# One order function for two phase changes of a hybrid encoder block on one Trainium2 core

## The chip, the cores and the metric

The kernel runs on one core of a Trainium2 chip. A core has five engines that run side by side, each with a queue of its own that it works off in order: TensorE (PE, the matrix unit; its weight loads are shown apart as PEld), VectorE (DVE), ScalarE (ACT), GpSimd (POOL) and SyncE (SP, which here issues the transfers). The metric is device time of one execution in microseconds (us). The kernel before took 1838.58 us, the median of three runs (1838.55 to 1839.45).

## The reference

One layer on 256 rows of width 2048: a half-weighted SwiGLU feed-forward part (FFN), a token mixer, and a second FFN, each with a modulated norm in front and a gated norm behind.

```python
h = modulate(rms_norm(x, ffn1_pre_g), sh1, sc1)
y = swiglu(h, ffn1_w_gu, ffn1_w_down)               # 2048 -> 2*5504 -> 2048
x = x + 0.5 * gt1 * rms_norm(y, ffn1_post_g)

h = modulate(rms_norm(x, mix_pre_g), sh2, sc2)
proj = h @ w_in                                     # q, k, v, u_b, v_b
out_a, out_b = band_attention(q, k, v), spatial_gating(u_b, v_b)
merged = concat(rms_norm(out_a, g_out_a), rms_norm(out_b, g_out_b))
y = merged @ w_out
x = x + gt2 * rms_norm(y, mix_post_g)

h = modulate(rms_norm(x, ffn2_pre_g), sh3, sc3)
x = x + 0.5 * gt3 * rms_norm(swiglu(h, ffn2_w_gu, ffn2_w_down), ffn2_post_g)
```

The modulation vectors (shift, scale and gate for each of the three parts) come from a product of a conditioning vector with `w_ada`.

## The kernel before

All products are made in split precision: an fp32 operand is split into a high part (`hi`, a cast on ScalarE) and the rest (`lo`, a subtraction on VectorE), and `mm3` (L111) issues three matmuls, high by high (L113), high by low (L114), low by high (L115). Weights stream in through `load` (L117, 1 MB each, three raw buffers) and `split` (L152), which puts each half of a load, a k-tile, into the next of a cyclic list of slots (`use_slots`, L138). A slot is free again when TensorE has used its k-tile for both tiles of rows. The 256 rows are two tiles, t = 0 and 1, of 128 rows. `h`, the normed and modulated input of a part, is split in the same way into hhi and hlo.

A phase change lies at the end of FFN 1 (`down_last`, L455, with `finish1`, L723) and at the end of the mixer's out-projection (L1007 to L1030). There the following has to happen for each tile of rows, in this order:

- TensorE ends the tile's last banks of `dn` (FFN 1) or `wo` (mixer). There are four banks of 512 columns per tile in FFN 1, of which each takes nine matmuls, and in the mixer two banks at the end, after two that were evacuated earlier.
- `evac` or `evac_b` adds a bank to `y` on VectorE (L479, L983). `y_done` (L296) squares it on ScalarE with its sum (L171) and multiplies it, in place, by the gate vector on VectorE (L303). In place, the product waits until the square has read `y`.
- `rstd` (L173) adds the sums on VectorE (ms) and takes the power on GpSimd (r).
- `post` (L309): four updates `x += y * r` on VectorE (L314) and four squares of x on ScalarE.
- `pre` (L271): again ms and r, then `dg`, a diagonal matrix of r (L277). TensorE transposes and scales x in four groups (`xtp`, L281). For each group VectorE makes the first quarter of h (L290) and ScalarE the other three (L288); then ScalarE makes hhi and VectorE hlo (L268, L269). Two PSUM banks hold the groups, so the third group waits until the first has been read.

Only then can TensorE begin the next product for that tile: `pj` (in-projection, `in_pair`, L736) or `gu` (FFN 2, `lead_chunk`, L356). For these, tile 0 leads: it takes eight k-tiles before tile 1 starts with the first (`LEAD`, L322). Some k-tiles of the next weight are split ahead, during the last matmuls of the phase before: six of `w_in` (`ahead1`, L708), five of `w_gu2` (L1017).

The order of the instructions on each engine is set by a scheduler at compile time: of the instructions that it believes ready, it takes the one of highest priority. `tc.high_priority()` raises that of the phase change. `after` (L125) adds an order between two instructions of one engine, and `order["split"]` holds pairs of instructions behind which the next splits have to stand (L160, L161):

```python
if t == 0:
    order["split"] += [(i_sq, i_x)] * 2        # post
...
if t == 0:
    order["split"] += [inst] * 2               # pre, for each group
```

Of the kernel before, what the change touches and what calls it, by code (L numbers as in the profile page):

```python
# [12 lines left out]
F32 = mybir.dt.float32  # L13
# [5 lines left out]
P = 128  # L19
# [43 lines left out]
def block_kernel(ctx: ExitStack, tc: tile.TileContext, a: dict, out: bass.AP):  # L63
# [46 lines left out]

    def mm3(ps, st, mv, start, stop):  # L111
        (ah, al), (wh, wl) = st, mv
        nc.tensor.matmul(ps, ah, wh, start=start, stop=False)  # L113
        nc.tensor.matmul(ps, ah, wl, start=False, stop=False)  # L114
        nc.tensor.matmul(ps, al, wh, start=False, stop=stop)  # L115

    def load(src, off, n):  # L117
        raw = wraw.tile([P, 2048], F32, tag="raw", name=nm("raw"))
# [1 line left out]
        return raw  # L120


    order = {"ada": (None, 0), "split": []}

    def after(inst, first):  # L125

# [25 lines left out]
    def split(raw):  # L152
        n = raw.shape[1]
        hi, lo = slot()
        i_hi = nc.scalar.copy(hi[:, :n], raw)  # L155
        i_lo = nc.vector.tensor_tensor(lo[:, :n], raw, hi[:, :n].bitcast(F32), op=ALU.subtract)  # L156
        order["last"] = (i_hi, i_lo)
        if order["split"]:
# [109 lines left out]
        i_hi = nc.scalar.copy(hi, h32)  # L268
        return i_hi, nc.vector.tensor_tensor(lo, h32, hi.bitcast(F32), op=ALU.subtract)  # L269

    def pre(i, x, t, ssq, h):  # L271

        hi, lo = h
        r = rstd(ssq)
        ts = slice(t * P, (t + 1) * P)
        dg = sm.tile([P, P], F32, tag="xn", name=nm("dg"), bufs=2)
        nc.vector.tensor_scalar(dg, ident, r, None, op0=ALU.mult)  # L277
        for j in range(4):
            ps = ptr.tile([P, 4, P], F32, tag="tr", name=nm("xtp"))
            for q in range(4):  # L280
                nc.tensor.matmul(ps[:, q, :], x[t][:, (4 * j + q) * P:(4 * j + q + 1) * P], dg, start=True, stop=True)  # L281
            h32 = sm.tile([P, 4, P], F32, tag="h32", name=nm("h32"), bufs=2)
            for q in range(4):
                kt = 4 * j + q
                g1 = gmul[:, i * KT + kt:i * KT + kt + 1]
                s1 = mod[:, SH[i] * KT + kt:SH[i] * KT + kt + 1]
                if q:
                    nc.scalar.activation(h32[:, q, :], ps[:, q, :], AF.Identity, bias=s1, scale=g1)  # L288
                else:
                    nc.vector.tensor_scalar(h32[:, q, :], ps[:, q, :], g1, s1, op0=ALU.mult, op1=ALU.add)  # L290
            inst = split_act(h32, hi[:, 4 * j:4 * j + 4, ts], lo[:, 4 * j:4 * j + 4, ts])
            if t == 0:
                order["split"] += [inst] * 2
        order["ada"] = (inst[1], 2)

    def y_done(t, n, y, ysq, g, junk, behind=None):  # L296

        ns = slice(n * CH, (n + 1) * CH)
        inst = square(junk, y[t][:, ns], ysq[t], n, D)
        if behind:  # L300
            after(inst, behind[0])
        r = rstd(ysq[t]) if n == 3 else None
        nc.vector.tensor_tensor(y[t][:, ns], y[t][:, ns], g[0][:, ns], op=ALU.mult)  # L303
        return r

    def new_ysq():
        return [new_sums("ysq", 4) for _ in range(NT)]

    def post(x, t, y, r):  # L309

        xsq = new_sums("xsq", 4)
        for j in range(4):
            js = slice(j * CH, (j + 1) * CH)
            i_x = nc.vector.scalar_tensor_tensor(out=x[t][:, js], in0=y[t][:, js], scalar=r, in1=x[t][:, js], op0=ALU.mult, op1=ALU.add)  # L314
            junk = sm.tile([P, CH], F32, tag="xn", name=nm("junk"), bufs=2)
            i_sq = square(junk, x[t][:, js], xsq, j, D)
        if t == 0:
            order["split"] += [(i_sq, i_x)] * 2
        return xsq


    LEAD = 8  # L322
# [1 line left out]
    def ffn(wgu, wdn, h, avp, ahp, plan, rate, gate_of, finish, lead=(), after_lead=(), ahead=None):  # L324
# [130 lines left out]
        def down_last(c, g):  # L455

            off, w = CHUNKS[c]
            nk = w // P
            ysq = new_ysq()
            blocks = []  # L460
            tail = ahead is None
            for i in range(nk):
                raw = load(wdn, D * off + i * P * 2048, 2048)
                tick()
                for q in range(2):
                    wh, wl = split(raw[:, q * 1024:(q + 1) * 1024])
                    blocks += [(wh[:, :CH], wl[:, :CH]), (wh[:, CH:], wl[:, CH:])]
            if not tail:
                ahead()

            def mm(t, n):
                ps = pmm.tile([P, CH], F32, tag="mm", name=nm("dn"))
                for k in range(nk):
                    mm3(ps, (stat[c][t][0][:, k, :], stat[c][t][1][:, k, :]), blocks[n * nk + k], k == 0, k == nk - 1)
                return ps

            def evac(t, n, ps):
                ns = slice(n * CH, (n + 1) * CH)
                nc.vector.tensor_tensor(y[t][:, ns], y[t][:, ns], ps, op=ALU.add)  # L479
                return y_done(t, n, y, ysq, g, avp.tile([P, CH], F32, tag="av", name=nm("junk"), bufs=2))  # L480

            with tc.high_priority():
                for n in range(4):
                    r = evac(0, n, mm(0, n))
                late = [mm(1, n) for n in range(4)]
                if not tail:
                    finish(0, y, r)
                for n in range(4):
                    r1 = evac(1, n, late[n])
                if tail:  # L490
                    finish(0, y, r)
                finish(1, y, r1)

        todo, ready = [], []
        if plan:
# [206 lines left out]
    h2, x1, sp1 = [], [], []  # L702
    if True:
        avp, gp = Lazy(tc, wx, "av1", 2), Lazy(tc, wx, "gp1", 1)
        ahs = ExitStack()
        ahp = Lazy(tc, ahs, "ah1", 2, lambda: (avp.open(), gp.open()))

        def ahead1():  # L708

            ahs.close()  # L710
            pre = wx.enter_context(tc.tile_pool(name="pre1", bufs=2))
            rest = ((adap, 2), (pre, 2), (wsp, 4), (wx1, 3))
            use_slots(*rest, once=((wx1, 1),) + rest)
            for _ in range(3):
                sp1.extend(in_visit())

        def gate1():
            flush_ada(SH[1])
            gain(1, 0, KT)
            x1.extend(load_x(a["x"]))  # L720
            return gate(0, 0.5, gp)

        def finish1(t, y, r):  # L723
            if not h2:
                h2.extend(new_h())
# [144 lines left out]
    with tc.tile_pool(name="bp", bufs=1) as bp:  # L870
# [74 lines left out]
        def wo_mm(ps, m, sp, kt, t, bs=(0, 1)):  # L945
            for b in bs:
                mv = (sp[0][:, b * CH:(b + 1) * CH], sp[1][:, b * CH:(b + 1) * CH])
                ts = slice(t * P, (t + 1) * P)
                mm3(ps[b][t], (m[0][:, kt, ts], m[1][:, kt, ts]), mv, kt == 0, kt == 7)
# [28 lines left out]
    with tc.tile_pool(name="gp2", bufs=1) as gp:  # L978
        ysq = new_ysq()

        def evac_b(t, n, ps, behind=None):
            ns = slice(n * CH, (n + 1) * CH)
            inst = nc.vector.scalar_tensor_tensor(out=y[t][:, ns], in0=ps, scalar=rb[t], in1=y[t][:, ns], op0=ALU.mult, op1=ALU.add)  # L983
            if behind:
                after(inst, behind[1])
            return y_done(t, n, y, ysq, g, sm.tile([P, CH], F32, tag="xn", name=nm("junk"), bufs=2), behind)

        use_slots((wsp, 4), (wx2, 3))
        g = []
# [17 lines left out]
        ps = wo_banks()  # L1007
        for kt in range(4):
            wo_mm(ps, m_b, sp[kt], kt, 0)
        sp += wo_visit() + wo_visit()  # L1010
        for b in range(2):
            for kt in range(4, 8):
                wo_mm(ps, m_b, sp[kt], kt, 0, (b,))

        use_slots((wsp, 1), once=((adap, 1), (wsp, 4)))
        sp3 = []
# [3 lines left out]
        for kt in range(4):  # L1020
            wo_mm(ps, m_b, sp[kt], kt, 1)
        for b in range(2):
            for kt in range(4, 8):
                wo_mm(ps, m_b, sp[kt], kt, 1, (b,))
        h3.extend(new_h())
        with tc.high_priority():
            for t in range(NT):
                for b in range(2):
                    r = evac_b(t, 2 + b, ps[b][t])
                pre(2, x2, t, post(x2, t, y, r), h3)  # L1030
    mxs.close()
    wx3 = ctx.enter_context(tc.tile_pool(name="wx3", bufs=3))

# [1 line left out]
    with ExitStack() as ahs:  # L1035
# [13 lines left out]
        def finish3(t, y, r):  # L1049
            for j in range(4):  # L1050
                js = slice(j * CH, (j + 1) * CH)
                nc.vector.scalar_tensor_tensor(out=x2[t][:, js], in0=y[t][:, js], scalar=r, in1=x2[t][:, js], op0=ALU.mult, op1=ALU.add)
# [79 lines left out]
```

## Time and profile before

| | |
|---|---|
| median of three runs | 1838.58 us |
| the profiled execution's own time | 1839.32 us |
| its span, first to last instruction | 1837.2 us |
| busy: PE, DVE, ACT, POOL | 1803.2, 1328.4, 854.5, 31.3 us |
| first phase change: last `dn` matmul, first `pj` matmul | 745.62, 752.78 us |
| second phase change: last `wo` matmul, first `gu` matmul | 1102.16, 1108.48 us |
| last `dn` matmul of FFN 2 | 1826.49 us |

The profile is of one execution, and its times count from the first instruction. Busy time of TensorE counts a matmul from its issue to its modelled end, and successive matmuls overlap. A row of the order of time gives start, duration, engine, line, operation, output and inputs with shapes, and how many instructions of the kind were merged; in square brackets stands for how long the engine was idle before, and what ended that.

### The profile page before, as it was taken

How to read it: one execution, taken by the hardware profiler on the slowest of the kernel's cores; microseconds unless marked ns; L12 is line 12 of the kernel's file. 1: busy time of each engine (PE TensorE's matmuls, PEld its weight loads, DVE VectorE, ACT ScalarE, POOL GpSimd, SP SyncE). 2: the span in 40 equal slices, each digit the busy share in tenths (PEclk: the TensorE clock that was granted, in tenths of full speed). 3: DMA queues.
4: the chain of work that ended last, by engine and by line, in shares of the span. 5: the costliest groups of instructions: out<-in, count | busy, mean ns of one | idle time of the engine just before them, and what ended most of it. 6: DMA issues, size and time to landing. Idle time of an engine off the chain costs nothing.

```text
span 1837.2 us, 21286 instructions
## 1 busy us (share of the span) xinstructions
PE 1803.2 (98%) x8271; PEld 1501.1 (82%) x8271; DVE 1328.4 (72%) x1481; ACT 854.5 (47%) x1105; POOL 31.3 (2%) x59
## 2 busy tenths in 40 slices
PE   7999999999999999999999999999999999999997
PEld 6777788888888898788888887888888888888896
DVE  7989998988877876768789986774445445445456
ACT  6544354444443344645555557444443443443342
POOL 0000000000000000000001000000000000000000
PEclk9999999999999999999999999999999999999999
DMA  9988788898888876479788974875555555555461
GB/s 395 385 335 318 286 320 342 326 367 332 336 335 321 329 289 261 172 276 358 292 307 326 382 291 165 332 305 187 195 191 187 196 191 187 196 190 186 160 250 70
DMA packets 71477, 499.11 MB, mean 272 GB/s; under 512 B 7968, under 2 KB 8144, under 8 KB 13136
## 3 DMA queue, kind: packets, MB, share of 16 engines
q1 hardware_dynamic: 70560, 492.48, 70.2%
q0 software_dynamic: 720, 5.24, 0.7%
q8 instruction: 65, 1.06, 0.2%
q14 instruction: 36, 0.29, 0.0%
q10 hardware_dynamic: 96, 0.02, 0.0%
HBM read 493.50 MB, written 4.22 MB: 271 GB/s over the span
## 4 chain that ended last, share of the span: by engine, by line
PE 93%; DVE 4%; ACT 1%; issue 1%; DMA 0%; POOL 0%; POOLq 0%; DVEq 0%; SPq 0%; ACTq 0%
PE gu L114 16%; PE gu L115 16%; PE gu L113 16%; PE dn L113 8%; PE dn L114 8%; PE dn L115 8%; PE pj L113 4%; PE pj L115 4%; PE pj L114 4%; PE wo L113 1%; PE wo L115 1%; PE wo L114 1%; DVE lo L156 1%; PE atp L418 1%; PE xtp L281 1%
## 5 line engine op out<-in xcount | busy, mean ns | idle before, releaser
L155 ACT CAST hi<-raw 128x1024 fp32r<-128x1024 f32 (+1 forms) x628 | 645.9, 1042 | 811.5 <-PE gu L115 422.6
L156 DVE TENSOR_TENSOR lo<-raw,hi 128x1024 fp32r<-128x1024 f32 (+1 forms) x628 | 747.8, 1208 | 380.9 <-ACT hi L155 379.5
L113 PE MATMUL gu<-hi,hhi 128*128 128x512 f32 (+1 forms) x1396 | 536.8, 387 | 8.9 <-DVE acc L392 4.2
L114 PE MATMUL gu<-lo,hhi 128*128 128x512 f32 (+1 forms) x1396 | 537.9, 385 | 0.4 <-DVE lo L156 0.3
L115 PE MATMUL gu<-hi,hlo 128*128 128x512 f32 (+1 forms) x1396 | 537.7, 385 | 0.0
L202 DVE CUSTOM_DVE_ANT_0 ada<-ada,c_bc,small 128x2048 f32<-128x2048 f32 x144 | 337.4, 2344 | 9.6 <-PE qkt L797 9.0
L113 PEld LDWEIGHTS gu<-hi,hhi 128*128 128x128 f32 x1396 | 262.4, 188 | 62.4 <-ACT hi L155 5.2
L114 PEld LDWEIGHTS gu<-lo,hhi 128*128 128x128 f32 x1396 | 263.0, 188 | 50.3 <-DVE lo L156 1.2
L115 PEld LDWEIGHTS gu<-hi,hlo 128*128 128x128 f32 x1396 | 262.9, 188 | 50.0
L113 PE MATMUL dn<-hi,ah 128*128 128x512 f32 x640 | 249.2, 389 | 0.0
L114 PE MATMUL dn<-lo,ah 128*128 128x512 f32 x640 | 249.0, 389 | 0.0
L115 PE MATMUL dn<-hi,al 128*128 128x512 f32 x640 | 249.0, 389 | 0.0
L113 PEld LDWEIGHTS dn<-hi,ah 128*128 128x128 f32 x640 | 120.1, 188 | 25.1
L115 PEld LDWEIGHTS dn<-hi,al 128*128 128x128 f32 x640 | 120.1, 188 | 25.0
L114 PEld LDWEIGHTS dn<-lo,ah 128*128 128x128 f32 x640 | 120.2, 188 | 24.8
L113 PE MATMUL pj<-hi,hhi 128*128 128x512 f32 x304 | 120.9, 398 | 0.0
L114 PE MATMUL pj<-lo,hhi 128*128 128x512 f32 x304 | 120.4, 396 | 0.0
L115 PE MATMUL pj<-hi,hlo 128*128 128x512 f32 x304 | 120.1, 395 | 0.0
L115 PEld LDWEIGHTS pj<-hi,hlo 128*128 128x128 f32 x304 | 57.1, 188 | 11.1
L114 PEld LDWEIGHTS pj<-lo,hhi 128*128 128x128 f32 x304 | 57.4, 189 | 10.7
L113 PEld LDWEIGHTS pj<-hi,hhi 128*128 128x128 f32 x304 | 57.4, 189 | 10.6
L453 DVE TENSOR_TENSOR y<-y,dn 128x512 f32<-128x512 f32 x64 | 41.9, 682 | 17.5 <-PE dn L115 17.5
(167 smaller groups left out, 1071.8 us busy)
## 6 DMA issues: line engine op xcount, KB each, us to landing
raw<-in_w_gu_dram SPq DMA_DIRECT2D x158, 1024.0 KB, 4.8
ada<-in_w_ada_dram SPq DMA_DIRECT2D x144, 1024.0 KB, 7.0
raw<-in_w_dn_dram SPq DMA_DIRECT2D x86, 1024.0 KB, 4.8
raw<-in_w_in_dram SPq DMA_DIRECT2D x40, 1024.0 KB, 6.2
raw<-in_w_out_dram SPq DMA_DIRECT2D x16, 1024.0 KB, 7.3
raw<-in_w_gu_dram SPq DMA_DIRECT2D x16, 768.0 KB, 5.3
x<-in_x_dram SPq DMA_DIRECT2D x4, 1024.0 KB, 7.5
gate<-gd POOLq DMA_DIRECT2D x3, 1024.0 KB, 8.4
```

The costliest lines, as they stand in the source:

```text
L113: nc.tensor.matmul(ps, ah, wh, start=start, stop=False)
L114: nc.tensor.matmul(ps, ah, wl, start=False, stop=False)
L115: nc.tensor.matmul(ps, al, wh, start=False, stop=stop)
L155: i_hi = nc.scalar.copy(hi[:, :n], raw)
L156: i_lo = nc.vector.tensor_tensor(lo[:, :n], raw, hi[:, :n].bitcast(F32), op=ALU.subtract)
L202: inst = nc.vector.tensor_tensor_reduce(out=st, in0=st, in1=c_bc, scale=1.0, scalar=bada[:, i:i + 1], op0=ALU.mult, op1=ALU.add, accum_out ...
L281: nc.tensor.matmul(ps[:, q, :], x[t][:, (4 * j + q) * P:(4 * j + q + 1) * P], dg, start=True, stop=True)
L418: nc.tensor.transpose(ps[:, q, :], av[:, q * P:(q + 1) * P], ident)
L453: nc.vector.tensor_tensor(y[t][:, ns], y[t][:, ns], ps[t], op=ALU.add)
```

## The change

Both phase changes go through one function, `change`, which lists the order of VectorE's and ScalarE's instructions for tile 0 and for tile 1's evacuation. Its parts are `y_part` (for `y_done`), `x_part` (for `post`) and `h_part` (for `pre`).

- The gate products go to `gy`: for tile 1 into the gate vector's own buffer, for tile 0 in place but for the last bank, which gets a small buffer. The products that go elsewhere need not wait for the square.
- The fourth square of x is made on VectorE.
- `chain` fixes the order: the last evacuation of tile 0, its product, the mean, four x, the fourth square, the mean, dg, and then the list `fill`. In `fill`, e, q and g are tile 1's add, square and product of a bank; v is VectorE's quarter of a group, a0 to a3 ScalarE's three activations and hhi, l hlo; H and L are hi and lo of k-tiles split ahead.
- All but the last two k-tiles that are split ahead must be split before the last evacuation of tile 0; those two stand in `fill`. Of the next four splits the first stands behind group 2 of tile 0, and three stand behind group 3.
- TensorE transposes groups 0 and 1 of tile 0 ahead of its last six `dn` or `wo` matmuls.
- At the first change the slots for the k-tiles ahead follow the cyclic list, which gives the first k-tile the slot that has been free for longest. At the second, tile 1's first two k-tiles of `wo` come earlier.
- Both x1 stores to memory are issued after both tiles.

```diff
-    def pre(i, x, t, ssq, h):
+    gy = {}
+    def y_part(t, n, y, ysq, g, junk):
+        ns = slice(n * CH, (n + 1) * CH)
+        if t:
+            gy[t, n] = g[0][:, ns]
+        else:
+            gy[t, n] = y[0][:, ns] if n < 3 else sm.tile([P, CH], F32, tag="xn", name=nm("gy"), bufs=2)
+        return (square(junk, y[t][:, ns], ysq[t], n, D),
+                nc.vector.tensor_tensor(gy[t, n], y[t][:, ns], g[0][:, ns], op=ALU.mult))
+    def x_part(t, x, y, ysq):
+        r = rstd(ysq[t])
+        on_dve, on_act = [order["mean"]], []
+        xsq = new_sums("xsq", 4)
+        for j in range(4):
+            js = slice(j * CH, (j + 1) * CH)
+            on_dve.append(nc.vector.scalar_tensor_tensor(out=x[t][:, js], in0=gy[t, j], scalar=r, in1=x[t][:, js], op0=ALU.mult, op1=ALU.add))
+            junk = y[t][:, js]
+            if j < 3:
+                on_act.append(square(junk, x[t][:, js], xsq, j, D))
+            else:
+                on_dve.append(nc.vector.tensor_tensor_reduce(
+                    out=junk, in0=x[t][:, js], in1=x[t][:, js], scale=1.0 / D, scalar=0.0,
+                    op0=ALU.mult, op1=ALU.add, accum_out=xsq[:, j:j + 1]))
+        r = rstd(xsq)
+        on_dve.append(order["mean"])
+        dg = sm.tile([P, P], F32, tag="xn", name=nm("dg"), bufs=2)
+        i_dg = nc.vector.tensor_scalar(dg, ident, r, None, op0=ALU.mult)
+        return dg, i_dg, on_dve, on_act
...
+    def change(i, x, y, ysq, h, first, tile1, splits, fill):
+        dg, i_dg, x_dve, x_act = x_part(0, x, y, ysq)
+        hs = h_part(i, 0, x, dg, h)
+        t1 = tile1()
...
+        dve, act = [[what[w] for w in f.split()] for f in fill]
+        chain(first[0], first[2], *x_dve[:-1], x_dve[-1], i_dg, *dve)
+        chain(first[1], *x_act, *act)
+        order["split"] += [(hs[2][2][-1], hs[2][1])] + [(hs[3][2][-1], hs[3][1])] * 3
+        dg, i_dg, x_dve, x_act = x_part(1, x, y, ysq)
+        h1 = h_part(i, 1, x, dg, h)
...
-            rest = ((adap, 2), (pre, 2), (wsp, 4), (wx1, 3))
-            use_slots(*rest, once=((wx1, 1),) + rest)
+            seven = [(next(slots["seq"]), 1) for _ in range(7)]
+            use_slots(seven[0], (adap, 2), (pre, 2), *seven[1:])
...
-        def finish1(t, y, r):
-            pre(1, x1, t, post(x1, t, y, r), h2)
-            nc.sync.dma_start(x_dram[t * P:(t + 1) * P, :], x1[t])
+        def finish1(y, ysq, first, tile1):
+            h2.extend(new_h())
+            after(first[0], ahead_sp[3][1])
+            after(first[1], ahead_sp[3][0])
+            hs = change(1, x1, y, ysq, h2, first, tile1, ahead_sp[4:],
+                        ("e0 e1 v0 e2 l0 L0 v1 l1 L1 e3 v2 l2 v3 l3 g0 g1 g2 g3",
+                         "H0 q0 a00 a01 a02 a03 H1 a10 a11 a12 a13 q1 q2 a20 a21 a22 a23 q3 a30 a31 a32 a33"))
+            after(order["dn"], hs[1][3])
+            for t in range(NT):
+                nc.sync.dma_start(x_dram[t * P:(t + 1) * P, :], x1[t])
...
+        for kt in range(2):
+            wo_mm(ps, m_b, sp[kt], kt, 1)
...
+            after(first[0], ahead_sp[2][1])
+            after(first[1], ahead_sp[2][0])
+            hs = change(2, x2, y, ysq, h3, first, lambda: [evac_b(1, 2 + b, ps[b][1]) for b in range(2)], ahead_sp[3:],
+                        ("e0 L0 v0 l0 v1 l1 L1 v2 e1 l2 v3 l3 g0 g1",
+                         "H0 a00 a01 a02 a03 a10 a11 a12 a13 H1 q0 a20 a21 a22 a23 q1 a30 a31 a32 a33"))
+            after(last[2], hs[1][3])
```

More of the change, by code (lines that the diff above doesn't have):

```diff
@@ L112, in mm3 @@
         (ah, al), (wh, wl) = st, mv
-        nc.tensor.matmul(ps, ah, wh, start=start, stop=False)
+        inst = nc.tensor.matmul(ps, ah, wh, start=start, stop=False)
         nc.tensor.matmul(ps, ah, wl, start=False, stop=False)
         nc.tensor.matmul(ps, al, wh, start=False, stop=stop)
+        return inst
     def load(src, off, n):
@@ L120, in load @@
         return raw
-    order = {"ada": (None, 0), "split": []}
+    order = {"ada": (None, 0), "split": [], "all": None}
     def after(inst, first):
@@ L157, in split @@
         order["last"] = (i_hi, i_lo)
+        if order["all"] is not None:
+            order["all"].append(order["last"])
         if order["split"]:
@@ L287, in pre @@
                 if q:
-                    nc.scalar.activation(h32[:, q, :], ps[:, q, :], AF.Identity, bias=s1, scale=g1)
+                    on_act.append(nc.scalar.activation(h32[:, q, :], ps[:, q, :], AF.Identity, bias=s1, scale=g1))
                 else:
[L290 to L319, printed above, removed]
+                    i_v = nc.vector.tensor_scalar(h32[:, q, :], ps[:, q, :], g1, s1, op0=ALU.mult, op1=ALU.add)
@@ L478, in evac @@
                 ns = slice(n * CH, (n + 1) * CH)
-                nc.vector.tensor_tensor(y[t][:, ns], y[t][:, ns], ps, op=ALU.add)
-                return y_done(t, n, y, ysq, g, avp.tile([P, CH], F32, tag="av", name=nm("junk"), bufs=2))
+                inst = nc.vector.tensor_tensor(y[t][:, ns], y[t][:, ns], ps, op=ALU.add)
+                return (inst,) + y_part(t, n, y, ysq, g, avp.tile([P, CH], F32, tag="av", name=nm("junk"), bufs=2))
             with tc.high_priority():
                 for n in range(4):
-                    r = evac(0, n, mm(0, n))
+                    first = evac(0, n, mm(0, n))
+                if tail:
+                    r = rstd(ysq[0])
                 late = [mm(1, n) for n in range(4)]
-                if not tail:
+                tile1 = lambda: [evac(1, n, late[n]) for n in range(4)]
+                if tail:
+                    tile1()
+                    r1 = rstd(ysq[1])
                     finish(0, y, r)
[L488 to L492, printed above, removed]
+                    finish(1, y, r1)
+                else:
+                    finish(y, ysq, first, tile1)
         todo, ready = [], []
@@ L948, in wo_mm @@
                 ts = slice(t * P, (t + 1) * P)
[L949 removed]
+                inst = mm3(ps[b][t], (m[0][:, kt, ts], m[1][:, kt, ts]), mv, kt == 0, kt == 7)
+            return inst
         def wo_banks():
@@ L985, in evac_b @@
                 after(inst, behind[1])
-            return y_done(t, n, y, ysq, g, sm.tile([P, CH], F32, tag="xn", name=nm("junk"), bufs=2), behind)
+            i_sq, i_gm = y_part(t, n, y, ysq, g, sm.tile([P, CH], F32, tag="xn", name=nm("junk"), bufs=2))
+            if behind:
+                after(i_sq, behind[0])
+            return inst, i_sq, i_gm
         use_slots((wsp, 4), (wx2, 3))
@@ L1019, in block_kernel @@
             sp3.append((raw, [split(raw[:, 1024 * q:1024 * (q + 1)]) for q in range(2 if p < 2 else 1)]))
[L1020 to L1024, printed above, removed]
+        order["all"] = None
+        for kt in range(2, 4):
+            after(wo_mm(ps, m_b, sp[kt], kt, 1), end0)
+        for kt in range(4, 8):
+            wo_mm(ps, m_b, sp[kt], kt, 1, (0,))
+        last = [wo_mm(ps, m_b, sp[kt], kt, 1, (1,)) for kt in range(4, 8)]
         h3.extend(new_h())
         with tc.high_priority():
[L1027 to L1030, printed above, removed]
+            for b in range(2):
+                first = evac_b(0, 2 + b, ps[b][0])
+            after(first[0], ahead_sp[2][1])
[4 more added lines that the diff above has]
+            after(last[2], hs[1][3])
     mxs.close()
```

38 lines of the change are left out of this document (27 added, 11 removed).

## The prediction

> **What bounds the kernel now.** I read the page's shares first, then who TensorE waited for at the two phase changes, then busy time by window, then the instructions in order of time.
>
> ```profile
> span 1837.2 us, 21286 instructions
> PE 1803.2 (98%) x8271; PEld 1501.1 (82%) x8271; DVE 1328.4 (72%) x1481; ACT 854.5 (47%) x1105; POOL 31.3 (2%) x59
> ```
> TensorE is busy for 98% of the span, and the change takes none of its work away. Only its idle time can be won. TensorE's waits from 744 to 775 us (end of the first FFN) and from 1100 to 1130 us (end of the mixer); columns are total, times, longest:
>
> ```profile
> PE xtp L281 <- issue: 2.3, 1, 2.3
> PE xtp L281 <- ACT hi L155: 0.8, 1, 0.8
> ...
> PE xtp L281 <- DVE dg L277: 1.8, 1, 1.8
> PE xtp L281 <- ACT h L288: 1.2, 1, 1.2
> PE xtp L281 <- ACT hi L155: 0.6, 1, 0.6
> ```
> All are in front of the transposing matmuls xtp: 3.1 us at the first change, 3.6 us at the second. The window rows (us, then busy time and count for PE, PEld, DVE, ACT, POOL, then granted clock):
>
> ```profile
> 746.00:770.00 24.00, 20.89 (x116) 18.05 (x116) 19.38 (x34) 19.71 (x46) 3.00 (x6) 0.93 0.55 207
> 1102.50:1124.00 21.50, 17.95 (x110) 15.54 (x110) 19.99 (x33) 20.98 (x47) 2.08 (x4) 1.00 0.47 166
> ```
> The first window also ran at a clock of 0.93: another 0.07 x 24.0 = 1.7 us. So the two changes cost about 3.1 + 1.7 + 3.6 = 8.4 us, which bounds what they can give. The other thing to see: VectorE is busy for 81% and 93% of these windows, ScalarE for 82% and 98%. Both feed TensorE, so they have little room, and a fixed order that makes one wait for the other loses room.
>
> The first change in order of time (start, us, engine, line, operation):
>
> ```profile
> 736.45 1.22 DVE L156 TENSOR_TENSOR lo<-raw,hi 128x1024 fp32r<-128x1024 f32 x1
> 738.79 0.68 DVE L479 TENSOR_TENSOR y<-y,dn 128x512 f32<-128x512 f32 x1
> 740.77 0.93 POOL L178 TENSOR_TENSOR r<-ms,mhalf 128x1 f32<-128x1 f32 x1 [52.86 <-DVE ms L176]
> 741.74 2.74 DVE L314 SCALAR_TENSOR_TENSOR x<-y,r,x 128x512 f32<-128x512 f32 x4 [0.46 <-POOL r L178]
> 745.62 0.39 PE L115 MATMUL dn<-hi,aw 128*128 128x512 f32 x1
> 746.26 1.21 DVE L156 TENSOR_TENSOR lo<-raw,hi 128x1024 fp32r<-128x1024 f32 x1
> 746.51 1.37 POOL L178 TENSOR_TENSOR r<-ms,mhalf 128x1 f32<-128x1 f32 x1
> 747.91 0.28 DVE L277 TENSOR_SCALAR dg<-ident,r 128x128 f32<-128x128 f32 x1 [0.44 <-POOL r L178]
> 748.30 4.73 PE L281 MATMUL xtp<-dg,x 128*128 128x128 f32 x24 [2.30 <-issue]
> 752.78 0.48 PE L113 MATMUL pj<-hi,hhi 128*128 128x512 f32 x1
> 755.08 0.41 DVE L290 TENSOR_SCALAR h<-xtp,gmul,mod 128x128 f32<-128x128 f32 x1
> 755.52 1.16 ACT L288 ACTIVATE h<-xtp,mod,gmul 128x128 f32<-128x128 f32 x3 [0.31 <-DVE h L290]
> 757.18 0.62 ACT L268 CAST hhi<-h 128x512 fp32r<-128x512 f32 x1
> 758.31 0.68 DVE L269 TENSOR_TENSOR hlo<-h,hhi 128x512 fp32r<-128x512 f32 x1
> 762.11 0.55 POOL L178 TENSOR_TENSOR r<-ms,mhalf 128x1 f32<-128x1 f32 x1
> 763.09 2.02 PE L281 MATMUL xtp<-dg,x 128*128 128x128 f32 x16 [0.81 <-ACT hi L155]
> 767.83 0.48 PE L113 MATMUL pj<-hi,hhi 128*128 128x512 f32 x1
> ```
> Tile 0 reaches TensorE at 748.30 and its projection starts at 752.78; tile 1's transposition starts at 763.09, and at 767.83 its projection can begin. ScalarE's three activations of a group start only when VectorE's quarter has ended (755.08 + 0.41, then 755.52): a group is a relay between the engines.
>
> **The change, part by part.** TensorE's step between matmuls of 512 columns is 8.16 / 36 = 0.227 us:
>
> ```profile
> 1094.00:1102.16 8.16, 8.16 (x37) 6.76 (x36) 1.54 (x3) 0.00 (x0) 1.00 0.38 129
> ```
> A k-tile takes 6 of them for one tile of rows: 1.36 us.
>
> (a) *First change, front.* Tile 0's last bank is done 36 steps before the last down matmul: 745.62 - 8.16 + 0.39 = 737.85. The fixed order takes the add at about 738.1 (a product may be running), the square on ScalarE beside the product, the root (0.93), four x updates (2.74), the fourth square on VectorE, the root (0.55), dg (0.28). For the fourth square I take 0.7 us: half of
>
> ```profile
> L644 DVE CUSTOM_DVE_ANT_0 junk<-x 128x1024 f32<-128x1024 f32 x2 | 2.4, 1222 | 1.5 <-DMA x<-in_x_dram 1.5
> ```
> and its read-out. With some 0.1 us at each handover: add 738.1, mean 739.5, x 740.8 to 743.4, square to 744.2, dg 745.1, transposition 745.4, against 748.30. It now stands ahead of the last six down matmuls, which TensorE reaches at 746.0 - 1.36 = 744.6, so 0.8 us of idle stays. Then two groups (2.02) and six matmuls (1.36) to 748.8. Meanwhile VectorE adds banks 0 and 1 (2 x 0.61), v0 ends at 747.0, three activations (1.16) and the copy (0.62) make the first hhi at 748.8. With the third group the projection starts at about 749.6: a lead of 3.2 us over 752.78. The root may take 0.55 to 1.37: the lead is 2.4 to 3.2.
>
> (b) *First change, fill.* The four groups follow as a relay: quarter 0.41, activations 1.16, copy 0.62, lo 0.68, and before the next quarter a weight split's lo (1.21): 4.1 us for each of the first two. VectorE idles while ScalarE works, since only listed instructions may stand there. v0 746.6, v1 750.5, v2 (another add) 755.1, v3 757.9 and with a square and the cast of k-tile 6 on ScalarE the last hlo ends at about 761.0, against 758.31 + 0.68 = 759.0. Only now come tile 1's four products (2.4), x (2.7), square (0.7) and root, dg (1.2, plus 0.5 for a weight lo that VectorE takes meanwhile): transposition at 768.5 against 763.09, and projection, with the same 4.7 as before less the 0.2 that a weight lo took there, at 773.0 against 767.83.
>
> How far TensorE got by then (pj, the first number in brackets; for gu at the second change the same):
>
> ```profile
> 746.00:767.82 21.82, 11.03 (x45) 8.25 (x46) 0.00 (x0) 0.92 0.58 219
> 1102.50:1121.09 18.59, 8.97 (x36) 6.56 (x37) 0.00 (x0) 0.00 (x0) 1.00 0.41 141
> ```
> Before: 45 matmuls of tile 0. After: at most 11 k-tiles, 66 matmuls, since there are eleven slots and tile 1 frees the first; 15.0 us from 749.6, and with three groups of transposing matmuls at about 0.9 (2.02 for two) done by 767.4, so TensorE idles for some 5 us in front of tile 1. Result: 773.0 - 767.83 = 5.2 later with 21 more done (4.8): **+0.4 us**. Bounds: -3.2 (the lead kept) and +5.2 (no more than the 45 done).
>
> (c) *Second change.*
>
> ```profile
> 1094.00 0.39 PE L115 MATMUL wo<-adas,mb 128*128 128x512 f32 x1
> 1095.70 0.75 DVE L983 SCALAR_TENSOR_TENSOR y<-wo,r,y 128x512 f32<-128x512 f32 x1
> 1104.32 2.05 PE L281 MATMUL xtp<-dg,x 128*128 128x128 f32 x16 [1.77 <-DVE dg L277]
> 1108.48 0.48 PE L113 MATMUL gu<-adas,hhi 128*128 128x512 f32 x1
> 1116.59 2.02 PE L281 MATMUL xtp<-dg,x 128*128 128x128 f32 x16 [0.58 <-ACT hi L155]
> 1121.10 0.48 PE L113 MATMUL gu<-hi,hhi 128*128 128x512 f32 x1
> ```
> Tile 0's last bank ends at 1094.4 and its evacuation waited until 1095.70. In the fixed order: evacuation 1094.5, mean 1096.0, x 1097.2 to 1099.9, dg 1101.5, transposition 1101.9 (0.7 us idle instead of 1.8). Bank 0's evacuation (0.75) and a weight lo (1.21) put v0 at 1103.5; hhi 1105.7, first gu 1106.05: a lead of 2.4 us. Fill: l0 1106.3, l1 1109.1, a split, v2 1110.5, last hlo to 1116.6; products 1.3, three x 2.0, square, root, dg: transposition 1122.3 against 1116.59, tile 1's gu 1126.8 against 1121.10: 5.7 later. Eleven k-tiles make 66 against 36, 30 x 0.227 = 6.8 us more: -1.1; the splits of k-tiles 6 to 10 queue behind the same VectorE order, so I take **-0.8 us**. Bounds -2.4 and +5.7.
>
> (d) *Tail.* In the chain that ended last:
>
> ```profile
> 1819.93 0.73 ACT junk L171 x2
> ...
> 1820.85 0.60 DVE y L303
> ...
> 1827.70 0.61 DVE y L479
> ```
> ```profile
> 1826.49 0.39 PE L115 MATMUL dn<-hi,aw 128*128 128x512 f32 x1
> ```
> TensorE is done at 1826.88, but the last add starts at 1827.70, since VectorE is full from 1820.69 on. With the product of (0, 3) in its own buffer it runs beside the square at 1819.9, and one 0.60 leaves the full stretch: **-0.6 us** (0 to -0.8).
>
> (e) *Moved or hidden.* K-tiles 0 and 3 are split before 738 in slots that are free then (the old first k-tile waited for a down slot, its lo at 746.26); the cover is VectorE's idle time before 738, and without it the first add is late by a lo, 1.21 us. Matmul counts stay. The two x1 stores go behind both tiles on SP's queue; a weight load behind one would be late by up to tile 1's delay, and I price that at nothing because eleven k-tiles need only loads issued earlier.
>
> Sum: +0.4 - 0.8 - 0.6 = -1.0. The profiled execution took 1839.32 us (span plus 2.1), 0.74 over the median of 1838.58; taken from the median, **1837.6 us**. A measurement here can tell 0.2%, 3.7 us, from no change.
>
> **The clock, row and rule.** An idle stretch of 2.3 us at 746 came with a clock of 0.93; at the second change 1.8 and 1.2 us did not. The piece of idle that I expect in front of tile 1, about 3 us at one go, could cost another 1.7. The Trainium skill, "TensorE: Matmul & The Clock Gate", section "Part 1: The HAM clock gate", says that the clock halves only after an idle window of about 3.4 us, in windows that run freely. By that rule my 3 us would cost nothing, as in the sum; by the row the sum would be 1839.3. The trace does not quite agree with the rule, since 2.3 us of idle was enough.
>
> **The rivals.**
> *Faster: the lead is kept.* Tile 1 comes early enough, because VectorE and ScalarE lose less in the relay than I laid out. For it: the listed order drops the weight splits that stood between. Against it: activations that wait for VectorE's quarter. It gives -3.2 - 2.4 - 0.6 = -6.2: 1832.4. It decides where tile 1's projection begins by about 768.2 (749.6 + 15.0 + 3.6).
> *Slower: TensorE's own order.* Its queue puts tile 1's transposition ahead of tile 0's later k-tiles, as at 762.3, where it stood idle for 0.8 us with projection behind it. With nothing more than 45 and 36 done, it is +5.2 + 5.7 - 0.6 = +10.3; with half of the 51 extra matmuls behind it +5: 1843. It decides when over 21 of the 51 stand behind.
> *The front does not come early:* the splits listed ahead of the first add are late (a load or a slot), so the lead of 5.6 us is gone while tile 1 is as late as forecast: 1837.6 + 5.6 = 1843.2. Against it: in the kernel before, five of the six k-tiles split ahead have their lo by 736.45 + 1.22 = 737.7 already; only the first comes at 746.26.
> *The clock dips again:* 1839.3.
>
> **How the numbers follow.** Forecast 0.37; clock dip 0.05 (also within 0.2%); lead kept 0.33; TensorE's order 0.20; late front 0.05. So same 0.42, faster 0.33, slower 0.25. The range for 8 in 10 runs from 1832, about the kept lead, to 1844.5, a little over the two slower cases; the forecast's own is 1835 to 1841.
>
> **What would show it.** Right: transposition of tile 0 at about 745.4 and 1101.9 with under 1 us of idle; tile 1's at 768 and 1122; in front of them TensorE idle for 3 to 6 us, waiting for a weight lo or for dg; the last add within 0.2 us of the last matmul's end; idle time of VectorE between the listed instructions. Wrong: tile 1's transposition before 764 and 1118, or TensorE idle at it with projection matmuls of tile 0 still to come.

## Result and profile after: 14 us slower, and where they went

The changed kernel takes 1853.38 us, the median of four runs (1852.22 to 1855.48), against 1839.01 us for the kernel before beside it (1838.55 to 1840.03): a ratio of 1.0079, 95% interval 1.0061 to 1.0096. A ratio here is not the quotient of the two medians, so it can differ a little from that. The profiled execution took 1853.27 us. The forecast was 1837.6, and no change.

The head of the page after:

```profile
span 1851.5 us, 21287 instructions
PE 1807.6 (98%) x8271; PEld 1501.6 (81%) x8271; DVE 1332.2 (72%) x1489; ACT 851.1 (46%) x1097; POOL 29.0 (2%) x59
```

TensorE's share is still 98%, and the whole-span shares show nothing of the 14 us. The waits of TensorE in the stretches of the two changes do (total, times, longest):

```profile
PE pj L114 <- DVE lo L157: 6.4, 2, 5.9
PE pj L113 <- ACT hi L156: 1.6, 2, 1.0
...
PE gu L114 <- DVE lo L157: 3.9, 2, 2.5
PE xtp L319 <- DVE dg L308: 3.4, 1, 3.4
```

Before, all waits stood in front of the transposition. Now the largest are for the lo of a weight. For one number per change I add up, over all matmul rows of a stretch, the time from one matmul's start to the next beyond its own step (0.227 us at 512 columns). From 720 to 800 us this lost time went from 7.0 to 16.3 us, in the stretch of the second change (1070 to 1190) from 4.6 to 11.2; in the rest of the span it fell by 1.0. With 0.7 won in the tail that makes 9.3 + 6.6 - 1.0 - 0.7 = 14.2 us, and the spans differ by 14.3.

The first change on VectorE and TensorE, in order of time:

```profile
745.79 2.02 PE L319 MATMUL xtp<-dg,x 128*128 128x128 f32 x16 [0.87 <-issue]
749.00 0.41 DVE L329 TENSOR_SCALAR h<-xtp,gmul,mod 128x128 f32<-128x128 f32 x1 [2.12 <-PE dn L114]
751.28 0.69 DVE L272 TENSOR_TENSOR hlo<-h,hhi 128x512 fp32r<-128x512 f32 x1 [1.28 <-ACT hhi L271]
751.57 0.48 PE L113 MATMUL pj<-hi,hhi 128*128 128x512 f32 x1
753.03 0.40 DVE L329 TENSOR_SCALAR h<-xtp,gmul,mod 128x128 f32<-128x128 f32 x1
755.30 0.69 DVE L272 TENSOR_TENSOR hlo<-h,hhi 128x512 fp32r<-128x512 f32 x1 [1.87 <-ACT hhi L271]
759.92 0.69 DVE L272 TENSOR_TENSOR hlo<-h,hhi 128x512 fp32r<-128x512 f32 x1 [1.88 <-ACT hhi L271]
761.49 1.22 DVE L157 TENSOR_TENSOR lo<-raw,hi 128x1024 fp32r<-128x1024 f32 x1 [0.48 <-ACT hi L156]
763.47 1.23 DVE L157 TENSOR_TENSOR lo<-raw,hi 128x1024 fp32r<-128x1024 f32 x1 [0.76 <-ACT hi L156]
764.61 0.68 DVE L272 TENSOR_TENSOR hlo<-h,hhi 128x512 fp32r<-128x512 f32 x1
765.22 2.49 DVE L285 TENSOR_TENSOR gate<-y,gate 128x512 f32<-128x512 f32 x4
767.62 2.73 DVE L297 SCALAR_TENSOR_TENSOR x<-gate,r,x 128x512 f32<-128x512 f32 x4
770.27 1.21 DVE L157 TENSOR_TENSOR lo<-raw,hi 128x1024 fp32r<-128x1024 f32 x1
771.54 0.80 PE L114 MATMUL pj<-lo,hhi 128*128 128x512 f32 x1 [5.85 <-DVE lo L157]
774.88 0.29 DVE L308 TENSOR_SCALAR dg<-ident,r 128x128 f32<-128x128 f32 x1 [0.44 <-POOL r L181]
775.22 2.70 PE L319 MATMUL xtp<-dg,x 128*128 128x128 f32 x16 [0.32 <-DVE dg L308]
779.63 0.48 PE L113 MATMUL pj<-hi,hhi 128*128 128x512 f32 x1
```

VectorE waits 1.28, 1.87 and 1.88 us inside the relay. The products and x updates of tile 1 come as one block of 5.05 us behind the last hlo (765.22 to 770.27). The lo of k-tile 7 stands behind that block, though TensorE had used its hi at 764.96 already, and TensorE idles for 5.85 us. Tile 1's transposition starts at 775.22 instead of 763.09, and at 779.63 its projection. Until then these matmuls of tile 0 were done (window, busy time and count for PE, PEld, ACT, then clock and transfers):

```profile
746.00:779.62 33.62, 15.92 (x55) 10.65 (x56) 0.00 (x0) 0.85 0.36 136
```

That closes the bill: tile 1 begins 11.8 us later with 10 more matmuls done than the 45 before (2.3 us), net 9.5, close to the 9.3 of lost time. The granted clock in this window is 0.85.

The second change, with all times about 8.3 us later than before by then (9.3 lost at the first change, 1.0 won outside it):

```profile
1102.24 0.75 DVE L1032 SCALAR_TENSOR_TENSOR y<-wo,r,y 128x512 f32<-128x512 f32 x1 [2.04 <-PE wo L115]
1102.91 1.22 DVE L157 TENSOR_TENSOR lo<-raw,hi 128x1024 fp32r<-128x1024 f32 x1
1102.95 0.39 PE L115 MATMUL wo<-adas,mb 128*128 128x512 f32 x1
1104.79 1.23 DVE L157 TENSOR_TENSOR lo<-raw,hi 128x1024 fp32r<-128x1024 f32 x1
1105.93 0.74 DVE L1032 SCALAR_TENSOR_TENSOR y<-wo,r,y 128x512 f32<-128x512 f32 x1
1113.11 2.51 PE L319 MATMUL xtp<-dg,x 128*128 128x128 f32 x16 [3.42 <-DVE dg L308]
1136.59 2.05 PE L319 MATMUL xtp<-dg,x 128*128 128x128 f32 x16
1141.28 0.47 PE L113 MATMUL gu<-adas,hhi 128*128 128x512 f32 x1
```

```profile
1110.00:1141.00 31.00, 15.19 (x59) 10.55 (x59) 0.00 (x0) 0.00 (x0) 0.94 0.36 126
```

The second fence is again a window, here of the gu matmuls: 59 of tile 0 until tile 1 begins at 1141.28. Here the front is late as well. Tile 0's last bank ends with the matmul at 1102.95, at 1103.34, but two weight lo (1.22 and 1.23 us) and a product stand ahead of its evacuation, which starts at 1105.93: 2.6 us after the bank's end, where it was 1.3 before. TensorE waits 3.42 us for dg where it waited 1.77.

### The profile page after: what moved, and what is told of

Same layout as the page of the kernel before. It is cut to its first block, busy times and chain, and to the rows that moved or that the text cites. A ratio compares the mean times of both kernels' runs of the same rounds, so it can differ in the third digit from the quotient of the medians.

```text
span 1851.5 us, 21287 instructions
## 1 busy us (share of the span) xinstructions
PE 1807.6 (98%) x8271; PEld 1501.6 (81%) x8271; DVE 1332.2 (72%) x1489; ACT 851.1 (46%) x1097; POOL 29.0 (2%) x59
## 4 chain that ended last, share of the span: by engine, by line
PE 92%; DVE 4%; ACT 2%; issue 1%; DMA 0%; POOL 0%; DVEq 0%; POOLq 0%; SPq 0%; ACTq 0%
PE gu L114 16%; PE gu L115 16%; PE gu L113 16%; PE dn L113 8%; PE dn L114 8%; PE dn L115 8%; PE pj L113 4%; PE pj L115 4%; PE pj L114 4%; PE wo L113 1%; PE wo L114 1%; PE wo L115 1%; DVE lo L157 1%; PE atp L453 1%; DVE ada L205 1%
```

## Experiments

All were timed against the kernel before. "Lost time" is the sum defined above, at the first and the second change.

**One change at a time.** Each kernel puts the functions of the kernel before back at one of the two phase changes.

> First change as in the kernel before, second change and tail as in the changed kernel. TensorE's lost time between its matmuls grew by 9.3 us at the first change and by 6.6 us at the second. If each loses by itself, this kernel takes about 1839.0 + 6.6 - 0.6 = 1845. Rival: the second change loses only because the first one left loads and slots late; then this kernel takes about 1838.4.

> Second change as in the kernel before, first change and tail as in the changed kernel. If each change loses by itself, about 1839.0 + 9.3 - 0.6 = 1847.7. Rival (the second loses because of the first): about 1853.

With the second change alone: 1846.46 us (before 1838.87), ratio 1.0035 (1.0022 to 1.0048), lost time 6.5 and 11.6. With the first alone: 1847.39, ratio 1.0045 (1.0033 to 1.0058), lost time 16.5 and 4.9. Each loses by itself, so the rival of both expectations falls, and the parts add up to the whole within the intervals.

**Which split stands ahead.**

```diff
-order["split"] += [(hs[2][2][-1], hs[2][1])] + [(hs[3][2][-1], hs[3][1])] * 3
+order["split"] += [(hs[1][2][-1], hs[1][1])] * 2 + [(hs[2][2][-1], hs[2][1])] + [(hs[3][2][-1], hs[3][1])] * 3
```

> The weight splits of k-tiles 6 and 7 may stand behind the second group's hlo and k-tile 8 behind the third's, instead of one behind the third and three behind the last; all else as in the changed kernel. Theory (TensorE starves in front of tile 1 because k-tile 7's lo stands behind four products and four x updates, 5.05 us, on VectorE): the wait of 5.9 us for that lo falls below 2 us, tile 1's transposition moves by no more than 1.2 us either way, and the time falls by 3 to 5 us to about 1849. Rival (the loss is that tile 1's transposition is late, whatever TensorE does meanwhile, because the matmuls done early are not missing later): the time stays within 1 us of 1853.4.

1851.08 us, ratio 1.007 (1.0056 to 1.0084). TensorE's waits at the first change:

```profile
PE pj L114 <- DVE lo L157: 4.9, 1, 4.9
```

Neither the theory nor the rival came out. The wait fell by 1 us only, since it moved to the next split behind the block, k-tile 9; tile 1's transposition came 2.6 us earlier (772.60), more than the 1.2 that the theory allowed. The lost time fell by 3.5 us at the first change and rose by 1.6 at the second, which has the same rule. As long as the block of 5 us stands where it does, some split has to stand behind it; whether another choice of splits does better was not run.

**The written order cut off behind dg.**

```diff
-chain(first[0], first[2], *x_dve[:-1], x_dve[-1], i_dg, *dve)
-chain(first[1], *x_act, *act)
+chain(first[0], first[2], *x_dve[:-1], x_dve[-1], i_dg)
+chain(first[1], *x_act)
```

> The written order ends at tile 0's diagonal matrix (and the squares of x) at both changes; what follows on VectorE and ScalarE is left to the planner. Free-buffer products, slots, early splits, the square on VectorE and TensorE's order of the six matmuls stay. Theory (the relay order with its idle waits makes tile 1 late): tile 1's transposition at the first change moves from 775.2 to 768 or earlier and the time falls to 1838 to 1845. Rival (the front is what loses: the transposition ahead of the last six down matmuls, whose first group is taken over only at 749.0): the time stays above 1850.

1842.48 us, ratio 1.0015 (1.0007 to 1.0024); lost time 6.2 and 9.2. TensorE's waits at the first change:

```profile
PE xtp L319 <- issue: 1.7, 1, 1.7
PE xtp L319 <- ACT h L327: 1.5, 1, 1.5
PE xtp L319 <- ACT hi L156: 0.8, 1, 0.8
```

No lo is waited for, and tile 1's transposition starts at 762.12: the theory. So the written fill costs about 10 us at the first change and 2 at the second.

**The same relay with tile 1's work in its gaps.**

```diff
-"e0 e1 v0 e2 l0 L0 v1 l1 L1 e3 v2 l2 v3 l3 g0 g1 g2 g3"
+"e0 e1 v0 e2 g0 l0 L0 v1 e3 g1 g2 l1 L1 v2 g3 l2 v3 l3"
-"H0 q0 a00 a01 a02 a03 H1 a10 a11 a12 a13 q1 q2 a20 a21 a22 a23 q3 a30 a31 a32 a33"
+"H0 q0 a00 a01 a02 a03 H1 q1 a10 a11 a12 a13 q2 q3 a20 a21 a22 a23 a30 a31 a32 a33"
```

> The changed kernel with one other written order at the first change: tile 1's four products stand in VectorE's waits of the relay (g0 ahead of l0, g1 and g2 ahead of l1, g3 ahead of l2), its last add ahead of l1, and its squares on ScalarE one group earlier, instead of all products behind l3. The second change keeps the order of the changed kernel. Theory (the order loses because VectorE idles in the relay, 1.3 + 1.9 + 1.9 us, while the work of tile 1 waits behind it): tile 1's transposition comes at 768 or earlier instead of 775.2, TensorE's loss there falls from 16.3 to under 9 us, and the time to 1844 to 1847. Rival (activations that wait for VectorE's quarter make the relay slow by itself): the transposition stays behind 772 and the time above 1850.

1847.77 us, ratio 1.0053 (1.0039 to 1.0067), a little over the range of the theory; lost time 8.8 and 12.1. On VectorE, around the third group:

```profile
753.23 1.29 DVE L285 TENSOR_TENSOR gate<-y,gate 128x512 f32<-128x512 f32 x2
754.60 0.69 DVE L272 TENSOR_TENSOR hlo<-h,hhi 128x512 fp32r<-128x512 f32 x1
...
758.08 1.42 DVE L297 SCALAR_TENSOR_TENSOR x<-gate,r,x 128x512 f32<-128x512 f32 x2 [0.66 <-POOL r L181]
759.41 0.69 DVE L272 TENSOR_TENSOR hlo<-h,hhi 128x512 fp32r<-128x512 f32 x1
```

The groups follow each other at much the same distances as in the changed kernel. The products and then, unlisted, the x updates fill the waits, and tile 1's transposition starts at 765.29, 10 us earlier. So most of the loss came from what the list kept out of its gaps: filling them wins 7.5 of the 16.3 us. The relay itself still costs something, since the order that was cut off loses 2.6 us less there (6.2).

**The six matmuls behind the transposition.**

```diff
-after(order["dn"], hs[1][3])
...
-after(last[2], hs[1][3])
```

> The changed kernel without the two rules that put the last six matmuls of the phase before behind tile 0's first two transposed groups. Theory (the take-over of the first group at 749.0, 3.2 us after its start, is the price of these six, since its end is signalled only with the fifth of them): the transposition starts 1.4 us later at the first change and is taken over within 1.7 us, at about 748.8, so the first change stays as it is; at the second the wait for dg falls from 3.4 to 2.0 us; together about 1852. Rival (the late take-over starts the whole delay of tile 1): 1849 to 1851.

1851.92 us, ratio 1.0072 (1.006 to 1.0085): the theory's number, but not for its reason. At 1.5 us under the changed kernel's median, it also lies within what these intervals can tell from that kernel. At the second change the wait for dg fell to 2.1 us as expected, and the third group then waited 1.3 us for ScalarE, so that the lost time there stayed at 11.2. At the first change the transposition did not start 1.4 us later (745.57 against 745.79), and its first group was taken over after 1.1 us:

```profile
746.66 0.41 DVE L329 TENSOR_SCALAR h<-xtp,gmul,mod 128x128 f32<-128x128 f32 x1 [0.32 <-PE xtp L319]
```

In the changed kernel that took 3.2 us (745.79 to 749.00) and the row names a down matmul as releaser. In the changed kernel's trace the group's own matmuls update no semaphore; the first update behind it is on the fifth of the six matmuls (748.57 to 748.96). Without the rule it is on the group's last matmul. The lost time there fell by 1.4 us, to 14.9.

**The rest of the second change.** In order of their runs: both front rules removed, with the cut-off order; then also the mixer's matmuls in their old order; then the splits held back.

```diff
# free_no_k2: cut-off order, without the six, and
-after(first[0], ahead_sp[2][1])
-after(first[1], ahead_sp[2][0])
# both_free: free_no_k2, and
-for kt in range(2):
-    wo_mm(ps, m_b, sp[kt], kt, 1)
...
-for kt in range(2, 4):
-    after(wo_mm(ps, m_b, sp[kt], kt, 1), end0)
+for kt in range(4):
+    wo_mm(ps, m_b, sp[kt], kt, 1)
# split_behind: second change of both_free (first as in first_unordered), and splits of k-tiles 1 to 4 issued after
+order["split"] += [(x_act[-1], i_dg)] * 4
```

> The kernel whose written order ends at tile 0's diagonal matrix (1842.5 us), also without the six matmuls behind the transposition and without the rule that k-tile 2 of the second change is split ahead of tile 0's last evacuation. Theory (the rest of the loss, 4.5 us at the second change, is its late front: a split of 1.2 us ahead of the evacuation and 1.4 us of matmuls behind the transposition): the wait for dg there falls from 4.7 to about 2.1 us and the time to about 1840. Rival (k-tile 2 is needed as early as that, or the loss lies in tile 1): the time stays at 1842 or more.

1837.3 us, ratio 0.9991 (0.9983 to 1.0), lost time 4.1 and 5.8. The wait for dg was 2.8, not 2.1, and the time was 2.7 us better than the theory's, of which the first change gave 2.1 (6.2 to 4.1). The two rules were taken out together, so the 3.4 us that the second change won (9.2 to 5.8) can't be divided between them.

> The kernel of 1837.3 us (both changes ordered only up to tile 0's diagonal matrix, no matmuls behind the transposition, no rule for k-tile 2), with the mixer's last matmuls in the order of the kernel before: tile 1's first two k-tiles stand behind tile 0's last bank again, 12 matmuls or 2.7 us more of work while the front runs. Theory (the wait for dg that is left at the second change, 2.8 us, comes from these matmuls being used up early): the wait falls below 1 us and the time to about 1835. Rival (tile 0's bank then ends 2.7 us later and the front with it; or the slots of these k-tiles come free later and their splits fall into the front): no gain, 1836.5 or more.

1837.25 us, ratio 0.999 (0.9981 to 0.9998), the same lost time, the same 2.8: the rival's number. But the run does not test the theory. In the trace of either kernel TensorE does the mixer's last matmuls in one and the same order, 34 of them behind tile 0's last bank (from 1091.09 to 1098.80 us in the one, from 1090.04 to 1097.74 in the other, at 0.227 us each). The edit of the program changed nothing there: the scheduler put out the same order from both. The changed kernel has 34 there too, and the kernel before 36.

> First change as in the kernel of 1835.13 us (nothing of its order written). Second change with free buffers, the order up to tile 0's diagonal matrix, and TensorE's order of the kernel before; only k-tile 0 is split ahead there, and the splits of k-tiles 1 to 4 are held back until dg is made. Theory (two splits of 1.2 us that stand on VectorE inside the front are why TensorE still waits 2.8 us for dg at the second change): the wait falls to about 0.4 us, and the time to 1832.5 to 1834. Rival (the splits held back are late for the first gate and up matmuls, or push tile 1's transposition): TensorE waits for a lo instead, and the time is 1835 or more.

1836.19 us, ratio 0.9984 (0.9975 to 0.9992), lost time 4.1 and 5.6. Its waits at the second change:

```profile
PE xtp L319 <- ACT h L327: 1.6, 1, 1.6
PE gu L114 <- DVE lo L157: 1.0, 3, 0.7
PE xtp L319 <- DVE dg L308: 0.9, 2, 0.7
```

The wait for dg fell, though to 0.9 and not to 0.4, and came back as waits for ScalarE and for lo, as the rival said. None of the three brought the second change below what kernels with the old second change lose there (4.6 to 5.6 us).

**What is good in the first change.** Three kernels keep the second change as it was before.

```diff
# first_free: cut-off order, without the six; first_unordered: also without
-chain(first[0], first[2], *x_dve[:-1], x_dve[-1], i_dg)
-chain(first[1], *x_act)
...
-after(first[0], ahead_sp[3][1])
-after(first[1], ahead_sp[3][0])
# slots_only: the kernel before, with
-rest = ((adap, 2), (pre, 2), (wsp, 4), (wx1, 3))
-use_slots(*rest, once=((wx1, 1),) + rest)
+seven = [(next(slots["seq"]), 1) for _ in range(7)]
+use_slots(seven[0], (adap, 2), (pre, 2), *seven[1:])
```

> First change with the written order up to tile 0's diagonal matrix only and without the six matmuls behind the transposition, products in free buffers, and the new slots and early splits; second change as in the kernel before; tail as in the changed kernel. TensorE's loss at the first change was 6.2 us with the free order against 7.0 before. Theory (the parts other than the written fill gain a little): about 1838.9 - 0.8 - 0.6 = 1837.5. Rival (free buffers, slots and early splits cost by themselves): 1840 or more.

1835.25 us, ratio 0.9983 (0.9974 to 0.9991), lost time 4.1 and 5.1; tile 1's transposition at 759.89, 3.2 us earlier than before.

> The kernel of 1835.25 us (second change as before, first change without the fill and without the six matmuls behind the transposition) with nothing written of the order at the first change: the chain up to tile 0's diagonal matrix and the rules for k-tile 3 are dropped too. What stays are the products in free buffers, the fourth square on VectorE, the squares' targets and the slots. Theory A (the written front earns its part: VectorE's and ScalarE's order brings dg early): the time goes up by 1.5 us or more, to 1836.8 to 1838. Theory B (the gain of 3.5 us comes from the free buffers, the square and the slots): it stays at 1835.3 within 0.8.

1835.13 us, ratio 0.9979 (0.997 to 0.9988), lost time 4.1: theory B. The chain up to dg and the rules for k-tile 3 earn nothing that these runs can show. (The rules for the four splits behind groups 2 and 3 stay in both kernels and were not tried by themselves.)

> The kernel before with one edit: the slots that k-tiles 0 to 10 of the first change take, in the changed kernel's order, so that the first k-tile does not have to wait for a slot of the down blocks. In the kernel before its lo (1.21 us) stood between the mean of x and dg, with the root on GpSimd taking 1.37 us beside it, and TensorE waited 2.3 us for the transposition. Theory (this split alone is what the better versions gain at the first change): its lo stands ahead of tile 0's first add, dg comes 1.2 to 2 us earlier, TensorE's loss at the first change falls from 7.0 to about 5 us, and the time to 1835.5 to 1837. Rival (the free buffers and the square on VectorE are what shortens the front): 1838 or more.

1836.52 us (before 1839.44), ratio 0.9987 (0.9978 to 0.9996), lost time 4.5 and 5.1. These two lines alone bring 2.9 us by the medians. GpSimd and TensorE at the first change:

```profile
746.48 0.55 POOL L178 TENSOR_TENSOR r<-ms,mhalf 128x1 f32<-128x1 f32 x1
747.51 1.96 PE L281 MATMUL xtp<-dg,x 128*128 128x128 f32 x16
```

The first k-tile's lo no longer stands in the front, and the wait of 2.3 us ahead of the transposition is gone, with the half clock that followed it (the granted clock from 740 to 760 us is 1.00). Against their own runs of the kernel before, the versions with free buffers are 0.6 to 0.9 us faster still (3.5 and 3.8 us by the medians), which the intervals can't tell from nothing. The best versions run here, 1835.1 to 1835.3 us, beat both kernels, by about 0.2% over the kernel before.

## Why the prediction was wrong, step by step

(a) *Front at the first change: right up to the transposition, wrong in what it led to.* The transposition started at 745.79 (forecast 745.4) after 0.87 us of idle (0.8). But v0 was to start at 746.6 and started at 749.00, because the end of the group was signalled on the fifth of the six matmuls behind it, which the sum put at nothing. The projection started at 751.57 instead of 749.6, and the lead was 1.2 us, not 3.2.

(b) *Fill at the first change: the step that failed.* It let TensorE's idle time in front of tile 1 be paid back by 21 matmuls done early, and put tile 1 only 5.2 us late. The idle time came about as forecast (5.85 us in front of tile 1, against some 5), but the matmuls that were to pay for it did not. The relay was there as laid out, 4.0 us from v0 to v1 (4.1 forecast), and so was the sequence hlo, products, x, dg. Three things were mis-sized. The last hlo ended at 765.3 instead of 761.0: 2.4 us came from v0, the rest from two weight lo ahead of it, the second of which belonged to k-tile 10, on which no rule lay. From there to dg it took 9.6 us instead of 7, because three weight lo, not one, were taken meanwhile. And I set the 66 matmuls by the eleven slots; what set them was VectorE. With lo 7 behind the block only 55 were done. So tile 1 was 11.8 us late with 10 extra matmuls done, not 5.2 with 21, and the term was +9.3 instead of +0.4. That is beyond its upper bound of +5.2 too, since the bound took tile 1's lateness from the forecast. The price that I gave to idle in front of tile 1 was 5 us, and I let it be covered by work whose splits queue on the engine that is late.

(c) *Second change.* The front was to be 2.4 us early. It was no faster than before: dg starts 9.4 us after the end of tile 0's bank (1103.34 to 1112.76; 9.6 before, 7.1 by the forecast), because two weight lo, k-tile 2's by the new rule, stood ahead of the evacuation. Behind the bank TensorE had 28 matmuls to do ahead of the transposition instead of 36, six of the eight by the rule that puts them behind it (1.4 us), and it waited 3.42 us instead of 0.7. Tile 1's transposition at 1136.59 is 11.7 us later than before, less the shift of 8.3; the forecast had 5.7. The term was +6.6, not -0.8, again beyond its bound. By the runs the fill makes 2.0 of it (11.2 to 9.2) and the two front rules 3.4 (9.2 to 5.8); the cause of the last 1.2 over the kernel before (5.8 against 4.6) stays open.

(d) *Tail: the size right, half of it by another way.*

```profile
1829.44 0.86 POOL L178 TENSOR_TENSOR r<-ms,mhalf 128x1 f32<-128x1 f32 x1 [7.57 <-DVE ms L176]
...
1841.45 0.39 PE L115 MATMUL dn<-hi,aw 128*128 128x512 f32 x1
...
1842.31 0.61 DVE y L516
...
1844.05 0.55 POOL L181 TENSOR_TENSOR r<-ms,mhalf 128x1 f32<-128x1 f32 x1 [7.52 <-DVE ms L179]
```

From the last matmul's start to the span's end it took 10.7 us before (1826.49 to 1837.2) and 10.05 now (1841.45 to 1851.5): -0.66 against a forecast of -0.6. The last add starts 0.47 us after TensorE's end, not within 0.2; before it was 0.82, so the named way gave 0.35. The other 0.31 came from the last root, which took 0.86 us before (first row, the kernel before) and 0.55 now (last row), since no product runs beside it any more. That the sum met the forecast is in part luck.

(e) *Hidden work: right for the stores and k-tiles 0 and 3* (TensorE waited for no load at the changes). *Missing: k-tile 2* of the second change, whose lo stood in the path.

*The rivals.* "The lead is kept" is what the first change does once nothing of it is ordered: 1835.1, though most of the gain comes from the slots (2.9 us with them alone), not from the relay. "TensorE's own order" did not decide by its own sign: of the 51 extra matmuls 33 were done ahead (10 and 23 by the rows), so 18 stood behind, under the 21. "The front does not come early" held at the second change, by the order that was written, not by a missing load. The clock dipped too: row and rule are below. I had listed these as alternatives; two of them came together, on top of the failed step.

## What to carry to other kernels

A written order for two engines is a promise that nothing else is worth doing in its gaps. Before writing one, list what the engine did in those gaps until then, here tile 1's products and x updates, and give it a place in the list, or end the list where the first wait on the other engine begins. And when an idle stretch is to be covered by extra work, ask which engine has to prepare that work: if it is the late one, the cover is late too.

## What the runs showed of the hardware

**The clock.** The pieces of a trace in which the granted clock is 0.50 are 3.41 us long or a multiple (but for the last, which the end of the program cuts), and they stand on one grid in each run. Three pieces of it, from three kernels (the window, its length, PE busy time and count, clock, transfers; rows of one fence follow each other):

```profile
745.33:748.74 3.41, 1.11 (x7) 1.00 0.84 327
748.74:752.16 3.42, 3.42 (x17) 0.50 0.75 292
```

```profile
1111.12:1114.54 3.42, 1.44 (x12) 1.00 0.00 0
1114.54:1117.95 3.41, 3.41 (x12) 0.50 0.59 185
```

```profile
1095.72:1099.13 3.41, 2.41 (x11) 1.00 0.23 96
1099.13:1102.54 3.41, 1.65 (x14) 1.00 0.01 2
1102.54:1105.95 3.41, 2.21 (x17) 1.00 0.64 214
```

The first is the kernel before: 2.3 us of idle inside one interval, and the next runs at half clock. The second is the second change of the changed kernel: its 3.42 us of idle are cut by the grid, 2.0 of them lie in this interval (2.1 counted from matmul start to matmul start), and half clock follows. The third is the kernel with both changes free: 2.76 us, cut into 1.0 and 1.8, and no half clock. Counting by matmul starts over the fourteen kernels (from 60 us on), every full-clock interval with 2.1 us or more without work was followed by half clock, 17 in all, and none with 2.03 or less; of three at 2.05, one was. The Trainium skill, "TensorE: Matmul & The Clock Gate", section "Part 1: The HAM clock gate", gives a free-running window of about 3.4 us, and the grid agrees. It asks for an idle window; here 60% of one was enough, and the measurement decides. So the row that I set against this rule was the better guide: by the rule the second change's 3.42 us, which fill no interval, would have cost no clock. In the changed kernel this made 10.2 us of half clock at the first change (766.4 to 776.6), where the kernel before had 3.4. TensorE was idle until 771.54 in it; the seven matmuls and the first transposed group after that took about 2.2 us longer than at full clock (steps of 0.43 instead of 0.227 us), which is part of the 9.3.

**The root on GpSimd.** It takes 0.55 us alone, and longer when it starts while VectorE runs an instruction with two inputs from SBUF. In the changed kernel, the two roots of the first change's x sums, the second one beside the lo that runs from 773.23 to 774.44:

```profile
744.82 0.55 POOL L181 TENSOR_TENSOR r<-ms,mhalf 128x1 f32<-128x1 f32 x1
773.48 1.36 POOL L181 TENSOR_TENSOR r<-ms,mhalf 128x1 f32<-128x1 f32 x1
```

That lo had 0.96 us left when the root started, and the root took 0.40 more than that. The same holds for the 65 roots of the fourteen traces that began beside a product, a hlo or a lo and took up to 1.47 us: each lasted 0.40 to 0.43 longer than that instruction had left. Beside an add that reads a PSUM bank the root took 0.55 (746.48 in the run with the slots alone). The prediction left this as a range of 0.55 to 1.37; what decides is the neighbour. The Trainium skill, "Advanced Engine Details and Errata", section "GPSIMD Details", says that GpSimd shares a read and a write interface with VectorE and conflicts with VectorE instructions that have two SBUF inputs; the rows agree.
